# One of nine buffers for the weights' low parts is placed 64 bytes off the distance that all others keep to the moving operands

## The chip, the cores and the metric

The kernel runs on one core of one Trainium2 chip. The metric is device time in microseconds of one execution; the figure before is the median of three runs, 2857.33 us (2853.26 to 2857.62). The profile comes from one more execution, which took 2856.76 us and has a span of 2855.0 us from its first to its last instruction.

## The reference, cut to what matters

Two different transformer blocks, each of two layers, follow one another on 256 tokens of width 1024, in float32. Each layer adds half of a feed-forward network, a mixer, and half of another feed-forward network:

```python
x = x + 0.5 * swiglu(rmsnorm(x, g1), w_in, w_out)     # D_FF = 2816
x = x + hybrid_mixer(rmsnorm(x, gm), ...)
x = x + 0.5 * swiglu(rmsnorm(x, g2), w_in2, w_out2)
```

The first block's mixer is a gated delta rule (8 heads) and a stick-breaking attention; the second block's is a latent attention, a block-sparse attention and a dilated attention, joined by gates. Nearly all of the arithmetic is in the products with dense weight matrices; some 459 MB of weights are read, each once.

## The kernel before, in words

The activations lie transposed: a tile of 128 partitions holds 128 of the 1024 features, and its 256 columns are the tokens. A dense product is done in three products of parts. Every float32 operand is split into a high part `hi` of the type float32r and a low part `lo` that holds what is left, and the kernel computes high times high, low activations times high weights, and high activations times low weights (`mm3`, lines 616 to 621). Each of these is one TensorE matmul: a 128x128 block of the weights is loaded into the array, and 256 columns of activations stream through it. In the rows a name such as `dn<-xh,lo` says: the result goes to the PSUM tile `dn`, the moving operand is `xh`, the weights are `lo`. A token-side product (`dense_tok`, line 648) has the roles swapped: there a block of the activations is loaded as weights, and the pieces of the weight matrix stream (`dn<-hi,xh`).

The weights come in through `Stream` (line 292). A plan made ahead lists the columns in the order of their use. They are loaded by DMAs of 512 KB into four `raw` buffers and cut into pieces of 512 columns of floats. For each piece `Stream.split` (line 336) takes a buffer `hi` and a buffer `lo`, nine of each in turn, and `Net.split` (line 527) fills them: ScalarE or VectorE makes `hi`, VectorE or GpSimd makes `lo`, as a small model of the engines' free times (`Clock`, line 233) says at build time. A piece is split seven pieces ahead of its use. For 256 columns of a matrix, one piece serves 12 matmuls in a row, four with `lo`; a column product loads `lo` twice, four other matmuls lie between, and it loads `lo` twice again. In the down projections (`acc<-ah,lo`) the four loads of one `lo` follow one another.

The order of the work on each engine is written out by the program. In the mixers, background generators (heads of the attentions) are stepped between the matmuls of the dense products. The feed-forward networks have no background work, and TensorE runs through each of them without a break.

Places in SBUF follow the order in which tiles are first asked for. `Net.skip` (line 413) asks for a tile that nobody uses, so that what comes after it lies farther up. Four such skips stand in the code before, of 480 and 448 bytes. In the program that was built, all moving operands of ordinary products (`xh`, `xl`, `ah`, `al`, `oh`, `mh` and so on) start at 448 bytes modulo 512, and all `hi` and `lo` buffers, each 2048 bytes, at 0 modulo 512. Between a weights' address and a moving operand's address there are therefore 64 bytes modulo 512 everywhere; in the token-side products, with swapped roles, 448.

Of the kernel before, what the change touches and what calls it, by code (L numbers as in the profile page):

```python
# [9 lines left out]
R = mybir.dt.float32r  # L10
# [9 lines left out]
PIECE, PIECE_AHEAD, PIECE_BUFS = 512, 7, 9  # L20
# [271 lines left out]
class Stream:  # L292
# [43 lines left out]
    def split(self, upto):  # L336
        while self.nsplit < min(upto, len(self.pieces)):
            u = self.nsplit
            i, c0, c1, r, o = self.pieces[u]
            self.load(r + RAW_BUFS)  # L340
            n = c1 - c0
            self.hi[u] = self.net.t([128, n], "hi", PIECE_BUFS, R, pool=self.pool)
            self.lo[u] = self.net.t([128, n], "lo", PIECE_BUFS, R, pool=self.pool)
            self.net.split(self.hi[u], self.lo[u], self.raw[r][:, o:o + n])
            self.nsplit += 1

# [38 lines left out]
class Net:  # L385
# [823 lines left out]
    def mix2(self, part, nxt):  # L1209
# [9 lines left out]
        with self.scope("heads"):  # L1219
# [15 lines left out]
            cq = tmp[:, 0:2]  # L1235
            v.tensor_mul(cq, pcq, rbc)
            cqs = split(cq, S("q_norm_2"), 2, "cq")
            sqc = tmp[:, 2:5]
            nc.scalar.activation(sqc[:, :2], cq, AF.Square)
            v.tensor_add(sqc[:, 0], sqc[:, 0], sqc[:, 1])  # L1240
            ck = tmp[:, 5:6]
            v.tensor_mul(ck[:, 0], ps[:, 0], self.r)
            cks = split(ck, S("kv_norm_2"), 1, "ck")
            nc.scalar.activation(sqc[:, 2], ck[:, 0], AF.Square)
            rp = slice(64, 96)
# [348 lines left out]
```

## Time and profile before

| | us |
|---|---|
| median of three runs | 2857.33 |
| the profiled execution's own time | 2856.76 |
| its span | 2855.0 |
| TensorE busy (22692 matmuls) | 2699.1 (95%) |
| VectorE busy | 2066.1 (72%) |
| ScalarE busy | 1387.9 (49%) |
| GpSimd busy | 750.3 (26%) |

Busy times of different engines lie beside one another. A TensorE instruction's duration is longer than the distance between the starts of two of them, since matmuls are pipelined; the pace is read from counts in a window. Line 228 stands in every row because one helper records all operations; the tiles' names tell them apart.

### The profile page before, as it was taken

The page shows a single profiled execution, that of the slowest core. Times are in us where ns is not written, and L with a number is a line of the kernel's source. Part 1 is how long each engine was busy: PE and PEld are TensorE (multiplying, and loading weights), DVE is VectorE, ACT ScalarE, POOL GpSimd, SP SyncE. Part 2 cuts the span into 40 slices and gives each one's busy share as a digit, 9 for nine tenths or more (in the row PEclk, how much of TensorE's full clock was granted, in tenths as well). Part 3 has the DMA queues.
Part 4 walks back from the last instruction along what each step waited for, and adds up shares of the span by engine and source line. Part 5 has one row for each costly group of instructions (what it writes and reads, how often), then busy time and mean ns, then how long its engine had stood idle before and what let it go on. Part 6 is the DMA issues. An engine that isn't in the chain of part 4 may idle for free.

```text
span 2855.0 us, 57792 instructions
## 1 busy us (share of the span) xinstructions
PE 2699.1 (95%) x22692; PEld 2650.5 (93%) x22692; DVE 2066.1 (72%) x3749; ACT 1387.9 (49%) x2761; POOL 750.3 (26%) x625
## 2 busy tenths in 40 slices
PE   8997897999999978889999999899999999999998
PEld 8997887999999978789999999889999999889998
DVE  6668888576676688894766767767766767767766
ACT  5454455544454544455444545445544545545543
POOL 0016555770010265557600102222000002221000
PEclk9998898999999989999999999999999999999999
DMA  6543233356555532333555654434555554435553
GB/s 220 185 164 134 103 111 111 126 169 205 197 192 190 178 115 104 113 117 134 173 199 190 210 194 167 145 133 167 185 193 181 193 192 155 145 124 183 188 184 126
DMA packets 128146, 463.48 MB, mean 162 GB/s; under 512 B 14336, under 2 KB 14592, under 8 KB 127744
## 3 DMA queue, kind: packets, MB, share of 16 engines
q1 hardware_dynamic: 127872, 459.78, 47.6%
q8 instruction: 178, 2.92, 0.4%
q14 instruction: 96, 0.79, 0.1%
HBM read 458.67 MB, written 1.05 MB: 161 GB/s over the span
## 4 chain that ended last, share of the span: by engine, by line
PE 74%; DVE 19%; ACT 3%; issue 2%; DMA 1%; POOL 1%; DVEq 0%; SPq 0%; ACTq 0%; POOLq 0%
PE dn L228 52%; PE acc L228 22%; DVE ssum L228 2%; DVE lo L228 1%; DVE dv L228 1%; DVE d_N L228 1%; DVE hi L228 1%; DVE dk L228 1%; DVE dq L228 1%; DVE d_prod L228 1%; DVE d_Ub L228 1%; DMA raw<-in_w_dram 1%; DVE xl L228 1%; ACT hi L228 1%; DVE d_dec L228 1%
## 5 line engine op out<-in xcount | busy, mean ns | idle before, releaser
L228 POOL TENSOR_TENSOR lo<-raw,hi 128x512 fp32r<-128x512 f32 (+2 forms) x502 | 663.9, 1342 | 1791.8 <-ACT hi L228 834.9
L228 ACT ACTIVATE hi<-raw 128x512 fp32r<-128x512 f32 (+2 forms) x1562 | 894.1, 618 | 344.7 <-PE dn L228 227.7
L228 DVE TENSOR_TENSOR lo<-raw,hi 128x512 fp32r<-128x512 f32 x1250 | 836.9, 709 | 163.7 <-ACT hi L228 154.8
L228 PE MATMUL dn<-xh,hi 128*128 128x256 f32 x4208 | 858.2, 286 | 6.9 <-DVE hi L228 6.1
L228 PE MATMUL dn<-xl,hi 128*128 128x256 f32 x4208 | 840.0, 281 | 4.8 <-DVE xl L228 4.8
L228 PE MATMUL dn<-xh,lo 128*128 128x256 f32 x4208 | 836.8, 280 | 4.7 <-DVE lo L228 4.7
L228 PEld LDWEIGHTS dn<-xh,hi 128*128 128x128 f32 x4208 | 650.3, 191 | 17.6 <-issue 9.1
L228 PEld LDWEIGHTS dn<-xl,hi 128*128 128x128 f32 x4208 | 650.4, 192 | 6.6 <-DVE xl L228 6.6
L228 PEld LDWEIGHTS dn<-xh,lo 128*128 128x128 f32 x4208 | 648.9, 191 | 5.5 <-DVE lo L228 5.5
L228 PE MATMUL acc<-al,hi 128*128 128x256 f32 x1408 | 198.5, 278 | 0.0
L228 PE MATMUL acc<-ah,hi 128*128 128x256 f32 x1408 | 198.4, 278 | 0.0
L228 PE MATMUL acc<-ah,lo 128*128 128x256 f32 x1408 | 198.3, 278 | 0.0
L228 ACT ACTIVATE ah<-us 128x512 fp32r<-128x512 f32 x88 | 55.7, 633 | 288.5 <-DVE us L228 288.5
L228 PEld LDWEIGHTS acc<-ah,lo 128*128 128x128 f32 x1408 | 178.4, 188 | 0.0
L228 PEld LDWEIGHTS acc<-al,hi 128*128 128x128 f32 x1408 | 178.3, 188 | 0.0
L228 PEld LDWEIGHTS acc<-ah,hi 128*128 128x128 f32 x1408 | 178.2, 188 | 0.0
L228 ACT ACTIVATE gs<-gs 128x512 f32<-128x512 f32 x88 | 55.8, 634 | 232.1 <-DVE gs L228 232.1
L228 PE MATMUL dn<-hi,xh 128*128 128x256 f32 (+2 forms) x640 | 139.3, 299 | 2.8 <-DVE k L228 2.8
L228 DVE TENSOR_TENSOR gs<-dn,nr 128x512 f32<-128x512 f32 x88 | 60.8, 691 | 107.9 <-PE dn L228 107.6
L228 DVE TENSOR_TENSOR us<-dn,nr 128x512 f32<-128x512 f32 x88 | 60.7, 690 | 107.2 <-PE dn L228 107.2
L228 PE MATMUL dn<-lo,xh 128*128 128x256 f32 (+2 forms) x640 | 130.4, 285 | 3.2 <-DVE lo L228 3.1
L228 PE MATMUL dn<-hi,xl 128*128 128x256 f32 (+2 forms) x640 | 130.6, 285 | 0.0
(319 smaller groups left out, 3229.3 us busy)
## 6 DMA issues: line engine op xcount, KB each, us to landing
raw<-in_w_dram SPq DMA_DIRECT2D x853, 512.0 KB, 4.2
raw<-in_w_dram SPq DMA_DIRECT2D x14, 384.0 KB, 3.2
raw<-in_w_dram SPq DMA_DIRECT2D x4, 408.0 KB, 3.9
cmat<-in_cmat_dram SPq DMA_DIRECT2D x1, 1216.0 KB, 6.8
x<-in_x_dram SPq DMA_DIRECT2D x4, 256.0 KB, 5.4
out_dram<-x SPq DMA_DIRECT2D x4, 256.0 KB, 2.6
cmat<-in_cmat_dram SPq DMA_DIRECT2D x1, 648.0 KB, 7.3
raw<-in_w_dram SPq DMA_DIRECT2D x2, 272.0 KB, 3.0
```

The source lines that it names most:

```text
L228: return f(*args, **kw)
```

## The change

In `Stream.split`, the low part of every ninth piece (0, 9, 18, ...) goes to a buffer of its own, `lo_far`; the other pieces share eight buffers `lo`. The first time, 448 bytes are skipped ahead of `lo_far`, and 64 bytes behind it. `lo_far` then starts at 448 bytes modulo 512, like the moving operands (distance 0), and the eight `lo` buffers start at 0 modulo 512 as before (distance 64). What is computed, and in which order, stays.

```diff
             self.hi[u] = self.net.t([128, n], "hi", PIECE_BUFS, R, pool=self.pool)
-            self.lo[u] = self.net.t([128, n], "lo", PIECE_BUFS, R, pool=self.pool)
+            if u % PIECE_BUFS == 0:
+
+                if u == 0:
+                    self.net.skip(448, self.pool)
+                self.lo[u] = self.net.t([128, n], "lo_far", 1, R, pool=self.pool)
+                if u == 0:
+                    self.net.skip(64, self.pool)
+            else:
+                self.lo[u] = self.net.t([128, n], "lo", PIECE_BUFS - 1, R, pool=self.pool)
             self.net.split(self.hi[u], self.lo[u], self.raw[r][:, o:o + n])
```

## Rows read from the trace of the kernel before

**Rows 1.** The page: engines' busy time, and the chain that ended last by engine.
```profile
PE 2699.1 (95%) x22692; PEld 2650.5 (93%) x22692; DVE 2066.1 (72%) x3749; ACT 1387.9 (49%) x2761; POOL 750.3 (26%) x625
...
PE 74%; DVE 19%; ACT 3%; issue 2%; DMA 1%; POOL 1%; DVEq 0%; SPq 0%; ACTq 0%; POOLq 0%
```

**Rows 2.** The page: TensorE's granted clock in 40 slices, in tenths.
```profile
PEclk9998898999999989999999999999999999999999
```

**Rows 3.** Windows, TensorE: stretch, length, busy (matmuls), clock, DMA share, GB/s.
```profile
30.00:200.00 170.00, 170.00 (x1446) 1.00 0.55 184
...
1949.00:2031.00 82.00, 82.00 (x699) 1.00 0.52 175
2036.00:2218.00 182.00, 182.00 (x1548) 1.00 0.54 186
2224.00:2399.00 175.00, 175.00 (x1546) 1.00 0.57 194
2582.00:2664.00 82.00, 82.00 (x698) 1.00 0.54 176
2669.00:2840.00 171.00, 171.00 (x1454) 1.00 0.52 173
```

**Rows 4.** Groups in 2036 to 2218 us: count, busy us, mean ns, idle before.
```profile
L228 PE MATMUL dn<-xh,lo 128*128 128x256 f32 x340 | 67.7, 281 | 0.0
```

**Rows 5.** Groups in 2224 to 2399 us.
```profile
L228 PE MATMUL dn<-xh,lo 128*128 128x256 f32 x340 | 66.1, 276 | 0.0
```

**Rows 6.** Timeline, TensorE, around 2033 us: start us, duration, operation, count, [idle].
```profile
2033.07 0.59 PE L228 MATMUL dn<-ssum,ones 128*128 128x256 f32 x2
2033.32 0.59 PE L228 MATMUL dn<-xh,hi 128*128 128x256 f32 x2
```

**Rows 7.** Timeline, TensorE, around 810 us.
```profile
810.26 0.67 PE L228 MATMUL dn<-ssum,ones 128*128 128x256 f32 x2 [1.22 <-DVE ssum L228]
810.58 0.58 PE L228 MATMUL dn<-xh,hi 128*128 128x256 f32 x2
```

**Rows 8.** Windows in mixers: one of token products, two of ordinary ones.
```profile
1823.40:1829.20 5.80, 5.80 (x52) 1.00 0.09 35
...
1848.00:1853.60 5.60, 5.60 (x50) 1.00 0.05 16
...
1321.60:1327.00 5.40, 5.40 (x50) 1.00 0.28 97
```

**Rows 9.** The page's groups: low parts made, and used as weights.
```profile
L228 POOL TENSOR_TENSOR lo<-raw,hi 128x512 fp32r<-128x512 f32 (+2 forms) x502 | 663.9, 1342 | 1791.8 <-ACT hi L228 834.9
...
L228 DVE TENSOR_TENSOR lo<-raw,hi 128x512 fp32r<-128x512 f32 x1250 | 836.9, 709 | 163.7 <-ACT hi L228 154.8
...
L228 PE MATMUL dn<-xh,lo 128*128 128x256 f32 x4208 | 836.8, 280 | 4.7 <-DVE lo L228 4.7
...
L228 PE MATMUL acc<-ah,lo 128*128 128x256 f32 x1408 | 198.3, 278 | 0.0
```

**Rows 10.** Timeline, TensorE, 327 us: a token product, then an ordinary one.
```profile
327.11 0.40 PE L228 MATMUL dn<-lo,xh 128*128 128x256 f32 x2
327.35 0.40 PE L228 MATMUL dn<-xh,hi 128*128 128x256 f32 x2
327.58 0.39 PE L228 MATMUL dn<-xl,hi 128*128 128x256 f32 x2
327.81 0.39 PE L228 MATMUL dn<-xh,lo 128*128 128x256 f32 x2
```

**Rows 11.** Timeline, TensorE, 508 us: another such place.
```profile
507.93 0.40 PE L228 MATMUL dn<-lo,xh 128*128 128x256 f32 x2
508.16 0.41 PE L228 MATMUL dn<-xh,hi 128*128 128x256 f32 x2
508.40 0.39 PE L228 MATMUL dn<-xl,hi 128*128 128x256 f32 x2
508.63 0.39 PE L228 MATMUL dn<-xh,lo 128*128 128x256 f32 x2
```

## The prediction

> **What bounds the kernel now.** I read the page's busy times and its chain of waits first: TensorE is busy for 95% of the span and carries 74% of the chain that ended last [rows 1], at full granted clock in nearly all slices [rows 2]. So the time is the number of matmuls times the distance between two starts (the pitch), wherever TensorE has no gap. I then cut the long gapless stretches out of the span by windows. There are twelve of over 300 matmuls: eight feed-forward networks (FFN), the gate columns of the two second-block mixers, and the end of the two first-block mixers. In such a window the pitch is its length over its count, less 2.4 for the matmuls that began before it (one lasts about 0.28 us).
>
> That view shows two paces for the same work [rows 3]. Five stretches are slow: 182 us / (1548 - 2.4) = 117.8 ns, and 170, 82, 82 and 171 us give 117.8, 117.7, 117.9 and 117.8. Seven are fast; the one shown gives 175 us / (1546 - 2.4) = 113.4 ns. The granted clock is 1.00 in all of them, no idle time stands before any matmul, and the mix of operands is the same [rows 4, 5]; only the mean duration differs, 281 against 276 ns. So the difference of 4.4 ns is not supply, not the clock and not instructions. A pace, once taken, holds to the end of the stretch; it is chosen at the start. An FFN that is entered behind a slow stretch over a short break (two matmuls of the norm, no idle row) stayed slow [rows 6]; one entered after 1.22 us of idle time became fast [rows 7].
>
> Of the two paces I make this picture, which is an inference: while matmul i streams its moving operand from SBUF, the weights of matmul i+1 are read from SBUF, and the two reads run in one of two steady phases, one of which collides more. What depends on addresses shows in the token-side products. There the roles are swapped (activations are weights, the stream moves), so "weights minus moving" is 448 bytes modulo 512 in place of the usual 64. In the one shown 5.8 us / (52 - 2.4) = 117 ns [rows 8], and of all its pairs, counted in order of time, 94% have the slow pace against 39% of the 18,157 ordinary pairs. A short ordinary stretch can be either: 5.4 / 47.6 = 113 ns and 5.6 / 47.6 = 118 ns [rows 8].
>
> **The change part by part.** *Instructions, queues and waits*: nothing is added. A buffer of its own for pieces 0, 9, 18, ... and eight for the rest come free in the same order as nine in turn, so each low part waits for the same earlier readers; the planner's costs and its two engine choices see the same numbers. The two skips are never written. Cost 0; were a low part placed on another engine, 1342 ns on GpSimd against 709 ns on VectorE [rows 9] would stand beside TensorE, where the long stretches show no wait.
>
> *Addresses*: the ordinary moving operands start at 448 modulo 512, the weights at 0. After the change one low-part buffer starts at 448, that is, at distance 0; the other eight move by 448 + 64 = 512 bytes and keep 64. Everything allocated later moves by 512 too.
>
> *Loads at distance 0*: low parts are weights in 4208 + 1408 matmuls of the two main groups [rows 9] and some 670 others; a ninth of them, counted through the program's order 695, comes in 307 visits, nearly all of two loads in a row (column products) and 43 of four (down projections). In a gapless stretch a visit comes on average every 108 / 1.7 = 64 matmuls. No row shows such a visit. The nearest are the five places where a token product runs without a gap into an ordinary one: there the first ordinary weights are read while a low part moves, at distance 0. In the two shown, the last two token matmuls take 0.24 and 0.23 us [rows 10, 11], the slow pace or close to it. The next two, the first behind distance 0, take 0.23 and 0.24; in single nanoseconds it is 237 to 242 against 227 at the fast pace. Then the fast pace holds, in all five places (three positions in the program), though the token product before was slow.
>
> Price of a visit in a fast stretch: two loads at 117.6 - 113.3 = 4.3 ns and 13 ns behind them make 22 ns; four loads make 30. Bounds: nothing (no row has a pitch under 113.3 at full clock, so a gain over the fast pace is excluded) and twice that, if every load cost as much as the pair behind it.
>
> *What the visits do to the pace* is the term that decides. By the five places a passage through distance 0 ends in the fast phase. Then each of the five slow stretches turns fast at its first visit. They hold 1478, 730, 1582, 730 and 1492 matmuls, 6012 in all; 6012 x 4.44 ns = 26.7 us. Until the first visit, half of 108 matmuls in each of five as a cautious value, 5 x 54 x 4.44 = 1.2 us is lost. All twelve stretches pay 186 visits x 22 ns + 43 x 30 ns = 5.4 us, and the 78 other visits, in the mixers where other engines hold part of the chain, half of that price, 0.8 us. Sum: -26.7 + 1.2 + 5.4 + 0.8 = -19.3 us. A faster TensorE needs its data earlier: the fast stretches run at DMA share 0.57 against 0.54 [rows 3] without a wait, so nothing is late next. From the profiled execution's 2856.76 us this makes 2837.5, and with the 0.6 us by which the median of the three runs (2857.33) lies above it, 2838.
>
> [...]
>
> **The rivals.** *Visits drop fast stretches into the slow phase.* Place: the seven fast stretches, 8614 matmuls, which are never disturbed now; price 8614 x 4.44 = 38.2 us, and with some 3 us for visits the end is 2857 + 41 = 2898. If the outcome of a visit is as mixed as that of a start after a gap (of the ordinary stretches of eight or more matmuls 28 settle slow, 90 fast), only part of this comes. With a share f of the 14,626 long-stretch matmuls slow, the change is (14626 f - 6012) x 4.44 ns + 6 us: it decides from f = 0.32 on; f = 0.5 gives +12, 2869. For it: distance 0 itself looks like the slow pace, and a fast stretch meets it 136 times, always in the same phase, so one bad outcome would repeat. Against: the five places.
>
> *The slow phase survives the visits.* Two or four loads may be too few, as a slow stretch has kept its phase over the norm's two matmuls [rows 6]. Then the fast stretches pay 136 visits (3.3 us), the five nearly nothing, the mixers 0.8: +4.1, 2861.
>
> *The change does nothing*, since the address of one buffer is no part of the mechanism: the phase is set by the timing of the start alone. 2857. For it: both paces occur at one distance in neighbouring FFNs.
>
> **How the numbers follow.** Locks broken: 0.57, 2838, with its own range 2832 (visits free) to 2844 (visits at twice the price). Fast stretches fall: 0.24, 2863 to 2898. Slow phase survives: 0.12, 2861. Nothing: 0.07, 2857. A measurement of this kernel tells about 0.2%, 5.7 us, from no change (the three runs lie within 4.4 us, less than one FFN's 1582 x 4.44 = 7.0, so the same long stretches were probably slow in each). The first case is faster, the last two within the bound, the second slower, with a hundredth moved to slower for dearer visits in the third: 0.57, 0.18, 0.25. The range reaches from 2828, where shorter mixer stretches gain as well, to 2872, the lower third of the second case.
>
> **What would show it.** Windows over the five slow stretches: about 113.4 ns of pitch plus the visits, some 114, from the first hundred matmuls on. In the timeline, pairs of matmuls on the odd buffer at 0.235 us and a longer pair behind them, every ninth piece. The other seven should lose 0.4 to 0.6 us per FFN and stay at 276 ns. Wrong would be: a mean duration of 281 ns in a stretch that was fast, five stretches unchanged at 117.8, or visits that cost more than 60 ns each.

## The result, and the profile after

The changed kernel takes 2887.72 us (median of four runs, 2885.81 to 2890.54), the kernel before in the same comparison 2855.30 us (four runs, 2852.48 to 2857.62). The ratio is 1.0115, with a 95% interval of 1.0097 to 1.0132: some 32 us slower, where 19 us faster were forecast. The profiled execution of the changed kernel took 2887.75 us.

Little else of the page moved with it. TensorE's share, the chain and the number of matmuls are those of [rows 1]; only its busy time grew, by 37 us. The page of the changed kernel, busy times and chain:

```profile
PE 2736.0 (95%) x22692; PEld 2688.9 (93%) x22692; DVE 2064.9 (72%) x3749; ACT 1388.9 (48%) x2761; POOL 751.0 (26%) x625
...
PE 74%; DVE 19%; ACT 3%; issue 2%; DMA 1%; POOL 1%; DVEq 0%; SPq 0%; ACTq 0%; POOLq 0%
```

Windows in the changed kernel (columns as in [rows 3]); the second, third and sixth lie in networks that ran at 113.3 ns before, the others in stretches that were at 117.8:

```profile
30.00:200.00 170.00, 170.00 (x1445) 1.00 0.56 184
632.00:814.00 182.00, 182.00 (x1547) 1.00 0.55 187
820.00:992.00 172.00, 172.00 (x1462) 1.00 0.56 186
...
1975.00:2057.00 82.00, 82.00 (x699) 1.00 0.52 175
2062.00:2244.00 182.00, 182.00 (x1548) 1.00 0.55 186
2260.00:2431.00 171.00, 171.00 (x1454) 1.00 0.56 190
```

Every one of them is at 117.7 to 117.9 ns: 171 / (1454 - 2.4) = 117.8 in the last, whose counterpart in [rows 3] has 175 / 1543.6 = 113.4. The mean duration tells the same, 281 ns where [rows 5] has 276. Groups of the changed kernel in 2260 to 2431 us:

```profile
L228 PE MATMUL dn<-xh,lo 128*128 128x256 f32 x274 | 54.6, 281 | 0.0
...
L228 PE MATMUL dn<-xh,lo_far 128*128 128x256 f32 x36 | 7.2, 281 | 0.0
```

The timeline of the changed kernel shows the place where that network loses its pace (start, duration, operation, count; two matmuls to a row):

```profile
2256.12 0.39 PE L228 MATMUL dn<-xh,lo 128*128 128x256 f32 x2
2256.35 0.39 PE L228 MATMUL dn<-xh,hi 128*128 128x256 f32 x2
2256.58 0.39 PE L228 MATMUL dn<-xl,hi 128*128 128x256 f32 x2
2256.80 0.40 PE L228 MATMUL dn<-xh,lo_far 128*128 128x256 f32 x2
2257.04 0.40 PE L228 MATMUL dn<-xh,hi 128*128 128x256 f32 x2
2257.28 0.40 PE L228 MATMUL dn<-xl,hi 128*128 128x256 f32 x2
2257.51 0.40 PE L228 MATMUL dn<-xh,lo_far 128*128 128x256 f32 x2
2257.75 0.40 PE L228 MATMUL dn<-xh,hi 128*128 128x256 f32 x2
```

Up to the first `lo_far` the rows stand 0.22 to 0.23 us apart, from it on 0.23 to 0.24, and so to the end of the network. It is the first visit of the stretch, 81 matmuls after its start, and it falls between two matmuls: the single starts are 113, 114 and 113 ns apart, then 119, 118, 118 and 117.

Matched matmul by matmul, the two traces differ by 30.1 us from first to last start. The seven long stretches that were fast give 37.3 us (8621 gaps), the five others -0.1, the shorter ordinary ones 3.8 (their slow share goes from 28% to 52%), the token products 0.1; what stands in between gives 11.0 us back. Part of that is waiting: the span less TensorE's busy time is 155.9 us before and 149.9 after; where the rest comes from is not shown.

Of the seven, one did not lose its pace to a visit. The network that begins at 630 us was slow in this execution from its start, 81 matmuls ahead of its first visit; the window ends before that visit:

```profile
631.00:639.00 8.00, 8.00 (x70) 1.00 0.38 133
```

8 / (70 - 2.4) = 118 ns, so its 7.0 us of the 37.3 belong to the start, though a fast start would have met a visit after 81 matmuls. The other six were slow from their first visit on (for the one from 1609 us that was its fourth matmul). Two stretches that were slow before began fast here and lost it to a visit as well: the one from 28 us, and the one from 2611 us, which a first visit at its fourth matmul had left fast and which ran at 113.3 ns up to its next visit, 105 matmuls behind its start.

### The profile page after: what moved, and what is told of

It is laid out like the page before. It is cut to its first block, busy times and chain, and to the rows that moved or that the text cites. A ratio compares the mean times of both kernels' runs of the same rounds, so it can differ in the third digit from the quotient of the medians.

```text
span 2885.9 us, 57791 instructions
## 1 busy us (share of the span) xinstructions
PE 2736.0 (95%) x22692; PEld 2688.9 (93%) x22692; DVE 2064.9 (72%) x3749; ACT 1388.9 (48%) x2761; POOL 751.0 (26%) x625
## 4 chain that ended last, share of the span: by engine, by line
PE 74%; DVE 19%; ACT 3%; issue 2%; DMA 1%; POOL 1%; DVEq 0%; SPq 0%; ACTq 0%; POOLq 0%
PE dn L228 52%; PE acc L228 22%; DVE ssum L228 2%; DMA raw<-in_w_dram 1%; DVE dv L228 1%; DVE dk L228 1%; DVE d_N L228 1%; DVE lo L228 1%; DVE hi L228 1%; DVE dq L228 1%; DVE d_prod L228 1%; DVE d_Ub L228 1%; DVE d_dec L228 1%; DVE xl L228 1%; ACT hi L228 1%
## 5 line engine op out<-in xcount | busy, mean ns | idle before, releaser
L228 POOL TENSOR_TENSOR lo<-raw,hi 128x512 fp32r<-128x512 f32 (+1 forms) x449 | 595.4, 1345 | 1755.6 <-DVE lo L228 862.7
L228 DVE TENSOR_TENSOR lo<-raw,hi 128x512 fp32r<-128x512 f32 (+1 forms) x1108 | 751.9, 710 | 156.4 <-ACT hi L228 143.0
L228 PE MATMUL dn<-xh,lo 128*128 128x256 f32 x3748 | 751.2, 282 | 2.4 <-DVE lo L228 2.4
L228 PEld LDWEIGHTS dn<-xh,lo 128*128 128x128 f32 x3748 | 578.9, 190 | 2.8 <-DVE lo L228 2.8
L228 PE MATMUL acc<-ah,lo 128*128 128x256 f32 x1256 | 183.1, 281 | 0.0
L228 PEld LDWEIGHTS acc<-ah,lo 128*128 128x128 f32 x1256 | 163.1, 189 | 0.0
L228 DVE CAST hi<-raw 128x512 fp32r<-128x512 f32 x190 | 112.0, 599 | 8.8 <-DMA raw<-in_w_dram 7.1
```

The lines of the kernel that those rows point to most:

```text
L228: return f(*args, **kw)
```

## The experiments

The theory: the matmul stream has a fast and a slow phase, the distance between the addresses of weights and moving operand decides which of them a passage leaves behind, and at distance 0 it is the slow one. The rivals: the separate buffer or the shift of addresses behind it costs the time; or the phase comes from the start of a stretch alone.

**The separate buffer at the old distance (e1_far64).**

```diff
                 if u == 0:
-                    self.net.skip(448, self.pool)
+                    self.net.skip(512, self.pool)
                 self.lo[u] = self.net.t([128, n], "lo_far", 1, R, pool=self.pool)
-                if u == 0:
-                    self.net.skip(64, self.pool)
```

> The changed kernel with 512 bytes skipped ahead of the separate buffer and none behind it: the separate buffer, its reuse and all other addresses are those of the changed kernel, only its distance is 64 again. Theory (the distance of one buffer makes the loss): the time of before, 2855 us (2850 to 2860), with the same seven long stretches at 113.3 ns. Rival (the separate buffer or the shift of everything behind it by 512 bytes makes the loss): 2888 us, all long stretches at 117.8 ns.

Measured: 2856.01 us against 2859.56 us of the kernel before on the same chip, ratio 0.9995 (0.9963 to 1.0027). Windows of this kernel, the first and third in networks that were fast before, the second in one that was slow:

```profile
630.00:805.00 175.00, 175.00 (x1547) 1.00 0.58 194
2038.00:2220.00 182.00, 182.00 (x1547) 1.00 0.57 187
2226.00:2401.00 175.00, 175.00 (x1546) 1.00 0.59 195
```

113.3, 117.8 and 113.4 ns: the separate buffer and the shift cost nothing that this interval shows; the 64 bytes do. One detail missed: six of the seven stretches were fast again, and one (1404 to 1591 us) was slow in this execution though nothing in it is at another distance.

**One visit at distance 0 (e2_once).** The separate buffer gets 128 columns more, so that each use can choose its place in it; only the ninth part that falls into the middle of one fast network lies at distance 0.

```diff
+            if u % PIECE_BUFS == 0:
+                o_far = (self.far(u) - 64) % 512 // 4
+                self.lo[u] = self.net.t([128, PIECE + 128], "lo_far", 1, R, pool=self.pool)[:, o_far:o_far + n]
...
+    def far(self, u):
+        at = self.first[self.keys.index(((1, "ffn2", 0), "g", 6))]
+        return 0 if 0 <= u - at < PIECE_BUFS else 64
```

> As the kernel before, with one visit alone: the separate buffer stays at distance 64, but for one piece in the middle of the second feed-forward network of the first layer, where it lies at distance 0 (four loads, in two pairs). That network ran its 1582 matmuls at 113.3 ns before. Theory (one passage turns the fast phase slow and it stays so to the end of the stretch): this stretch runs at 113.3 ns up to the visit and at 117.8 ns behind it, some 750 matmuls later it ends, 3.3 us more; the next stretch, behind an idle time, is fast again; 2858 us in all. Rival (the stream falls back to the fast phase by itself between visits, and in the changed kernel the next visit comes before that): the pace is back at 113.3 ns within 100 matmuls, under 0.5 us more.

Windows of this kernel before and after the visit, then the timeline at it:

```profile
624.00:703.00 79.00, 79.00 (x700) 1.00 0.58 197
708.00:803.00 95.00, 95.00 (x809) 1.00 0.54 182
```

```profile
704.24 0.39 PE L228 MATMUL dn<-xh,hi 128*128 128x256 f32 x2
704.46 0.39 PE L228 MATMUL dn<-xl,hi 128*128 128x256 f32 x2
704.69 0.40 PE L228 MATMUL dn<-xh,lo_far 128*128 128x256 f32 x2
704.92 0.40 PE L228 MATMUL dn<-xh,hi 128*128 128x256 f32 x2
705.16 0.40 PE L228 MATMUL dn<-xl,hi 128*128 128x256 f32 x2
```

79 / (700 - 2.4) = 113.2 ns, then 95 / (809 - 2.4) = 117.8 ns for all of the 853 matmuls that are left. The pace goes with the first two of the four loads and does not come back in this network: the theory's case; the rival that the stream recovers falls. The expected total can't be tested with this one run (2855.81 us): its first network was fast, ahead of any visit at 0, and the network behind the visited one was slow although an idle time lies between them, both against expectation. Why a start takes one pace or the other is not shown.

**The distance by itself (m1_scan).** A kernel of nothing but matmuls, with these stretches for every distance `d`:

```python
out.append(("gap", [d] * 72))               # behind a wait of about 1 us
out.append(("fp32", [d] * 72))              # behind one float32 product, no wait
out.append(("zero", [0] * 20 + [d] * 72))   # behind distance 0, no wait
out.append(("gap", [64] * 36 + [d] * 2 + [64] * 48))              # visits
out.append(("zero", [0] * 20 + [64] * 24 + [d] * 2 + [64] * 48))
```

> This kernel leaves the whole network out: it only runs matmuls of 256 columns in float32r on constant tiles, in 160 stretches without a gap, and returns the input. The moving operands start at 448 modulo 512; the distance from them to the weights goes from 0 to 496 bytes in steps of 16. For each distance 72 matmuls are run behind a wait of about 1 us, 72 behind one float32 product without a wait, and 72 directly behind 20 matmuls at distance 0. Then, for each distance, a visit: two loads at it between stretches at 64, once from a start behind a wait and once behind 20 matmuls at distance 0. Theory (two phases; at distance 0 only the slow one exists, and a passage through it leaves the stream in the slow phase at distance 64 too): distance 0 gives 117.8 ns behind every start, 64 gives 113.3 behind a wait and 117.8 behind distance 0, and a visit at 0 turns a fast stretch slow. Rival (the phase comes from how the stretch starts, the address of a few loads is no part of it): the pitch of a start behind a wait is the same at all distances, and a visit at 0 leaves the pace as it was. No theory yet says which other distances can turn a slow stretch fast; the scan is to show whether there is one.

The steady pitch in ns, mean of the last 42 distances between starts in a stretch, by distance and start (from the starts of the single matmuls):

```
distance   0     16    32    48    64    80    96    112   128   144   160   176   192   208   224   240
wait      120.0 118.3 118.4 117.8 113.3 118.8 117.4 119.8 120.0 120.0 120.0 118.1 117.8 116.7 116.7 117.4
float32   120.0 118.4 118.4 117.8 117.8 120.0 118.7 119.9 118.5 118.3 120.0 118.1 117.8 116.7 116.7 120.0
from 0    120.0 118.3 118.4 118.3 117.8 118.8 117.3 120.0 118.7 118.3 120.0 118.1 113.3 116.7 116.7 120.0
```

From 256 to 496 the same numbers come again within 0.2 ns, but for 320 behind a wait (117.8, where 64 has 113.3). So the address does matter, with a period of 256 bytes; only 64 and 192 of these distances know the fast phase, and each of them the slow one too. At other distances, too, the pitch can depend on the start (144: 120.0 or 118.3). Distance 0 was expected at 117.8 and has 120.0. Of the visits from a fast stretch, those at 0, 16, 32, 224, 256, 288, 368 and 480 end slow; those at 192 and 448 cost nothing (0 ns over six pairs). From a slow stretch (117.8 ns), two loads at 192 or 448 end fast (113.3 ns), two at 0 or 256 leave it slow. Of the 32 visits from a stretch that distance 0 had made slow, 18 end fast, so 192 and 448 are not alone in that; what sets them apart is that they cost a fast stretch nothing. The timeline of this kernel shows both; first a visit at 0 out of the fast phase (its two loads are the row at 979.44), then one at 192 out of the slow phase (the row at 1261.77; 0.25 us to the next row, then 0.22):

```profile
978.99 0.39 PE L64 MATMUL dn<-xl,hi 128*128 128x256 f32 x2
979.21 0.39 PE L64 MATMUL dn<-xh,lo 128*128 128x256 f32 x2
979.44 0.40 PE L64 MATMUL dn<-xh,hi 128*128 128x256 f32 x2
979.67 0.40 PE L64 MATMUL dn<-xl,hi 128*128 128x256 f32 x2
979.91 0.40 PE L64 MATMUL dn<-xh,lo 128*128 128x256 f32 x2
```

```profile
1261.30 0.40 PE L64 MATMUL dn<-xh,lo 128*128 128x256 f32 x2
1261.53 0.40 PE L64 MATMUL dn<-xh,hi 128*128 128x256 f32 x2
1261.77 0.40 PE L64 MATMUL dn<-xl,hi 128*128 128x256 f32 x2
1262.02 0.39 PE L64 MATMUL dn<-xh,lo 128*128 128x256 f32 x2
1262.24 0.39 PE L64 MATMUL dn<-xh,hi 128*128 128x256 f32 x2
```

**Passages from each phase (m2_passages).** The same kernel with other stretches:

```python
PRE = [("gap", [64] * 36), ("zero", [64] * 36), ("gap", [192] * 36), ("zero", [192] * 36)]
for d in (0, 192, 64):
    for n in (1, 2, 4):
        out.append((how, ([0] * 20 if how == "zero" else []) + pre + [d] * n + [64] * 36))
```

> This kernel, too, leaves the network out and only runs stretches of matmuls of 256 columns. First part: a stretch in one of four steady paces (distance 64 behind a wait, 64 behind distance 0, 192 behind a wait, 192 behind distance 0), then 1, 2 or 4 loads at distance 0, 192 or 64, then 36 at 64; three times each. The prediction took token products (distance 448) that pass one load at 0 and then run fast at 64 as the model of a visit. Theory (the outcome depends on the phase that is left and on the count, so that model was the wrong one): from the fast phase at 64 two loads at 0 end slow (117.8 ns), as the scan showed; from the slow phase at 192 one load at 0 ends fast (113.3 ns). Rival (any passage through 0 from another distance than 64 ends as in the scan): slow from everywhere, and the five places of the trace owe their pace to something else. Second part: mixtures of 64 and 192; third: distances a few bytes beside 64 and 192. Expected for the mixtures: 113.3 ns behind every start, if a load at 192 costs nothing in the fast phase and ends the slow one (scan: 0 ns and 27 ns over six pairs). No theory says what 4 or 8 bytes do.

The pace before the passage is read from the trace, since a start behind a wait does not always take the same one. Counts of passages, and the pace over the last 20 matmuls at 64:

```
phase left        loads passed     ends at 113.3   ends at 117.8
fast at 64        1 or 2 at 0            0               4
fast at 192       1, 2 or 4 at 0         0              12
slow at 64        1, 2 or 4 at 0         0              14
slow at 192       1 or 2 at 0            6               0
fast at 64        2 or 4 at 192          6               0
slow at 64        1 at 192               0               6
slow at 64        2 or 4 at 192          6               0
```

None of these cells is mixed. One that the table leaves out is: 36 loads at 192 in the slow phase and then straight on at 64, with no load at 0, ended fast three times and slow six times, so the pace that is left and the distances do not settle every outcome. The passage that the prediction had read in the token products, out of the slow phase at 192 (448 is 192 in a period of 256), does end fast; from either phase at 64 the same loads at 0 end slow. The timeline of one such passage out of the slow phase at 192 (the load at 0 is the first of the row at 210.66; from 211.14 on the rows stand 0.22 to 0.23 us apart):

```profile
210.43 0.40 PE L68 MATMUL dn<-xh,lo 128*128 128x256 f32 x2
210.66 0.40 PE L68 MATMUL dn<-xh,hi 128*128 128x256 f32 x2
210.90 0.40 PE L68 MATMUL dn<-xl,hi 128*128 128x256 f32 x2
211.14 0.39 PE L68 MATMUL dn<-xh,lo 128*128 128x256 f32 x2
211.36 0.39 PE L68 MATMUL dn<-xh,hi 128*128 128x256 f32 x2
```

Theory confirmed, the rival falls. Of the mixtures, four loads at 64 and two at 192 (and the reverse) ran at 113.3 ns behind all nine starts each; sixteen and eight kept 117.8 behind a float32 product, three of nine, a miss. Distances of 52 and 76 had 113.3 behind each of their three starts, 60 and 68 had 118.3 and more: a few bytes matter.

**The separate buffer at 192 (e3_far192).** As e2_once, with another choice:

```diff
     def far(self, u):
-        at = self.first[self.keys.index(((1, "ffn2", 0), "g", 6))]
-        return 0 if 0 <= u - at < PIECE_BUFS else 64
+        return 192
```

> The changed kernel with the separate buffer at distance 192 in place of 0. In the scan two loads at 192 left a fast stretch fast at no cost and turned a slow one fast. Theory (the outcome of a visit decides the stretch): all twelve long stretches run at 113.3 ns from their first visit on; against before 6012 x 4.44 ns less some 1 us until the first visits, 25 us: 2830 to 2833 us where before is 2857. Rival (visits of the real kernel, with four loads in the down projections and other neighbours, end otherwise than in the scan): stretches that change pace several times, 2845 to 2870.

Measured: 2829.65 us against 2866.59 us of the kernel before on the same chip, ratio 0.9891 (0.9845 to 0.9937); the time is a little under the 2830 to 2833 that were expected. All twelve long stretches end in the fast phase. Windows in three that were slow in the profile before, and the timeline at the first visit of one that had started slow:

```profile
1955.00:2020.00 65.00, 65.00 (x576) 1.00 0.56 185
2040.00:2200.00 160.00, 160.00 (x1414) 1.00 0.58 195
2660.00:2815.00 155.00, 155.00 (x1371) 1.00 0.55 182
```

```profile
633.80 0.40 PE L228 MATMUL dn<-xl,hi 128*128 128x256 f32 x2
634.04 0.40 PE L228 MATMUL dn<-xh,lo_far 128*128 128x256 f32 x2
634.28 0.39 PE L228 MATMUL dn<-xh,hi 128*128 128x256 f32 x2
634.51 0.39 PE L228 MATMUL dn<-xl,hi 128*128 128x256 f32 x2
634.74 0.39 PE L228 MATMUL dn<-xh,lo_far 128*128 128x256 f32 x2
634.96 0.39 PE L228 MATMUL dn<-xh,hi 128*128 128x256 f32 x2
```

160 / (1414 - 2.4) = 113.3 ns; the same place has 117.8 in [rows 3]. One pair of loads was not always enough: two stretches (from 2025 and from 2648 us) stayed slow behind the first pair of a piece's loads and turned fast with the second. This is the change with another number: the same instructions, with the buffer 128 bytes beyond the common distance in place of 64 short of it.

**All low parts at 192 (e4_lo192).** Nine buffers as before, 128 bytes skipped ahead of them and 384 behind:

```diff
+            if u == 0:
+                self.net.skip(128, self.pool)
             self.lo[u] = self.net.t([128, n], "lo", PIECE_BUFS, R, pool=self.pool)
+            if u == 0:
+                self.net.skip(384, self.pool)
```

> The kernel before with all nine low-part buffers at distance 192 and all high parts at 64: every third pair of matmuls is a visit. Theory (loads at 192 cost nothing in the fast phase and end the slow phase): every ordinary stretch is fast within some ten matmuls, so that the short ones of the mixers gain as well; of 6997 slow pairs nearly all go, 6997 x 4.44 ns = 31 us at most: 2826 to 2831 where before is 2857. Rival (a steady mixture has phases of its own, and each change of distance costs its 20 to 27 ns): some 3100 changes in pairs add 60 us, above 2900.

Measured: 2828.38 us, ratio 0.9885 (0.9831 to 0.9940) to the kernel before. Of 18,192 ordinary pairs 5.3% are slow, against 39%. It is faster than the kernel before and the changed one; from the 2829.65 us of e3_far192 it can't be told apart. Its four runs lie within 3.2 us (2826.59 to 2829.79). A window of this kernel in the network that [rows 4] show slow, with 174 / (1538 - 2.4) = 113.3 ns:

```profile
2026.00:2200.00 174.00, 174.00 (x1538) 1.00 0.59 194
```

**One visit at 192 in a slow network (e5_once192).** As e2_once, for the key `((2, "ffn2", 0), "g", 6)` and 192 in place of 0.

> As the kernel before, with the separate buffer at distance 64 but for one piece in the middle of the second feed-forward network of the second block's first layer, where it lies at 192. That network ran its 1582 matmuls at 117.8 ns before. Theory (one visit at 192 ends the slow phase for the rest of the stretch): 117.8 ns up to it, 113.3 behind it, 3.3 us less in this stretch. Rival (the slow phase comes back): 117.8 ns again within 100 matmuls, under 0.5 us less.

Windows of this kernel before and after that visit:

```profile
2040.00:2131.00 91.00, 91.00 (x775) 1.00 0.57 193
2136.00:2218.00 82.00, 82.00 (x726) 1.00 0.55 183
```

91 / 772.6 = 117.8 ns, then 82 / 723.6 = 113.3 ns to the end of the network, 772 matmuls. The first two of the visit's four loads left it slow, the second two ended the slow phase. The theory's case; the one run's total, 2857.60 us, says nothing, since other stretches fell otherwise.

## Why the prediction was wrong

**The bound** was right: the two paces, 113.3 and 117.8 ns, and that a pace is kept to the end of a stretch. So was the cost of nothing for instructions, queues and waits (e1_far64; low parts stand 502 on GpSimd and 1250 on VectorE in the traces before and after the change).

**The step that failed** is "by the five places a passage through distance 0 ends in the fast phase". Those places leave the slow phase of a token product, at distance 448, by one load at 0. A visit leaves distance 64, by two or four loads. m2_passages ran both: the first ends fast, 6 of 6; from 64, fast or slow, it ends slow, 18 of 18. The five places were rightly read, but the outcome depends on where the passage comes from, not on distance 0 alone. The trace of before held no passage out of the fast phase at 64, the case that decided 8614 matmuls; five like cases from another phase were taken for it. In the sum, the term of -26.7 us for the five slow stretches came to -0.1, and the seven fast ones, for which it had only the price of the visits, lost 37.3 us.

**The rival that held** is the first, visits that drop fast stretches. It was priced at 38.2 us for the seven stretches, and they lost 37.3, 7.0 of it by a slow start; its 2898 was too far up by the 11 us that come back in between and by the 3 us for visits, less 3.8 us that the shorter stretches lost and that it did not count. A visit in the slow phase has next to no price: its loads are at 120.0 ns at most (the pitch at distance 0 in m1_scan) where the others are at 117.8, and the three long stretches that were slow from the start in both traces differ by under 0.1 us. Its ground, that one bad outcome would repeat in every network, was the right one, and the chance of 0.24 too small. The other rival, that the slow phase survives, holds for a settled slow phase at 64: 14 of 14 passages in m2_passages, and three of the five slow stretches, which began slow again and stayed so. The other two began fast and fell. So which stretches are slow differs between executions, and three runs within 4.4 us were too few to tell.

**The picture of the reads** is not settled. That addresses matter is shown: in m1_scan the distance alone moves the pitch behind a wait from 113.3 ns at 64 to 120.0 ns at 0, so the prediction's third rival, that the address of one buffer is no part of the mechanism, does not hold here. That reads of weights and moving operand collide in SBUF remains the author's inference: no run shows the reads themselves.

## What to carry to other kernels

Where TensorE runs without gaps, divide the length of windows by their counts, stage by stage: here the same work at two paces (113.3 and 117.8 ns), at one clock (1.00) and without waits, pointed to the addresses of weights and moving operands, and single-nanosecond gaps showed where the pace changes. Before a rare event is judged by its like in a trace, look whether the state it comes from is the same; where it is not, a kernel of matmuls alone tests every passage in one run. In this kernel loads at 192 bytes in every ninth piece ended the slow phase, with the first pair or a later one (117.8 to 113.3 ns, e3_far192), and two at 0 ended the fast phase (113.2 to 117.8 ns, e2_once).

## What the runs showed of the hardware that was not expected

The pitch of 256-column float32r matmuls depends on the distance between moving operand and weights with a period of 256 bytes (m1_scan, in steps of 16 bytes), from 113.3 to 120.0 ns, and at 64 and 192 it has two stable values, 113.3 and 117.8 ns. Which of them a stretch takes is not the same from one execution to the next: one network ran at 113.3 ns in the profile of the kernel before and at 117.8 in that of e1_far64, whose distances are the same. One network of 1582 matmuls is worth 7.0 us, and the kernel before spread from 2845.56 to 2876.57 us over its later runs; e3_far192 and e4_lo192, which end the slow phase themselves, spread over 5.7 and 3.2 us, and the changed kernel, whose visits end the fast phase, over 4.7. The fast phase ended once without any load at another distance: in a stretch of e2_once at 113.3 ns, the matmul at 1374.07 us started 132 ns behind the last, and the next ten starts were 117 to 119 ns apart; that the late start did it is not shown. Why the token products of e4_lo192 stay slow in 87% of their pairs, though their mixture of distances was fast in m2_passages, is open.
